# Branch B of a hybrid decoder layer: the odd head's keys copied out before the even head's split, and stored by ScalarE

## The chip, the core and the metric

The kernel runs on one NeuronCore of a Trainium2 chip. The engines are named as in the profile: PE is TensorE (PEld its weight loads), DVE is VectorE, ACT is ScalarE, POOL is GpSimd and SP is SyncE, which issues most of the DMA transfers; SPq and ACTq are the rows of DMAs issued by SP and by ACT. The metric is the device time of one execution in microseconds (us).

## The reference

One decoder layer over 1024 positions, 1024 wide, in f32. Branch B, where the change lies, is a latent attention with 8 heads:

```python
qb = (rmsnorm(cq, q_a_norm[l]) @ w_q_b[l]).reshape(B, S, N_HEADS_B, Q_HEAD_B)
kvb = (rmsnorm(ckv, kv_a_norm[l]) @ w_kv_b[l]).reshape(B, S, N_HEADS_B, KV_HEAD_B)
q_nope, q_rope = qb[..., :QK_NOPE], rope(qb[..., QK_NOPE:], positions)
k_nope, v_b = kvb[..., :QK_NOPE], kvb[..., QK_NOPE:]
k_rope = rope(kr[:, :, None, :], positions)[:, :, 0, :]
out_b = mla_attention(q_nope, q_rope, k_nope, k_rope, v_b)
merged = jax.nn.sigmoid(g_a) * (out_a @ w_o_a[l]) + jax.nn.sigmoid(g_b) * (out_b @ w_o_b[l])
x = x + rmsnorm(merged @ w_out[l], post_norm_mix[l])
h2 = rmsnorm(x, pre_norm_mlp[l])
y = jnp.square(jax.nn.relu(h2 @ w_up[l])) @ w_down[l]
x = x + rmsnorm(y, post_norm_mlp[l])
```

A head has 64 key columns of its own (`k_nope`) and 32 rotary ones that all heads share; scores are causal and scaled, and each softmax is over all earlier positions.

## The kernel before

Every f32 matrix is split into two parts, a high part (a cast on ACT, L83) and the rest (a subtraction, L84, mostly on DVE), and a product is three matmuls: L89 and L91 with the high part of the left operand, L90 with its low part. Tiles are 128 partitions by 512 or 1024 columns.

The order of work is the program text, reordered: the tile framework schedules each engine's row of instructions beforehand with a time model of its own (`schedule_with_timeline_sim=True`), and it puts in the waits. On the chip each engine then takes its row strictly in order. So a line moved in one function can move rows on every engine, and an instruction that waits holds up all that stand behind it on its engine.

In branch B `head_k` makes the keys of a pair of heads with one product: partitions 0 to 63 of the PSUM bank are the even head's keys, 64 to 127 the odd head's. The even head's half is split in place into `bkh` (ACT) and `bkl` (DVE). The odd head's half has to change partitions, so it goes through DRAM: ACT copies it into a `tmp` tile, a DMA stores that in `KN`, and `head_k` of the odd head loads `KN` into the low partitions of its `bkl` (L725) and splits it there (a cast on ACT, a subtraction on DVE). The shared rotary keys come by DMA too (`bkh<-krh`, `bkl<-krl`, L710). `tmp` has three buffers, shared with the query products (`scaled`, L252) and the gate products (`gate_out`, L450, stored to DRAM as `gate<-tmp`):

```python
def tmp():
    return tl(p1, [P, 512], F32, "tmp", 3)
```

PSUM is shared out by tags: `F` has one bank (gate products, and queries and keys of heads 1 to 7), `big` two tiles of two banks (scores, value projection, and queries and keys of head 0, `two_halves`), `T` two banks (transposed probabilities), `O` one. A tile of a tag can be written only when the one before it in the same buffer has been read.

A head's attention goes in steps `s` of two blocks of 128 queries: `attn_b_front` makes scores (L768 to L772), their maximum (L775, L776) and `e`, the exponentials (ACT, L778), which POOL divides by their sum (L781); `attn_b_back` of the step before transposes `e` (L797), splits it (`bth`, `btl`) and multiplies by the values (L805 to L808). Head h+1's keys and queries are made in step 2 of head h. Gate products (24 matmuls of 512 columns each) stand between as work that waits for little:

```python
NGATES = (3, 1, 2, 2, 2, 3, 3, 0)
```

After head 7 comes `merge`; it loads stored gates (`sg<-gate`, L910) and takes their sigmoid on ACT (L911), two of them already near the end of head 6. Exponential and sigmoid need different function tables on ACT, and an ACT_TABLE_LOAD row stands where they alternate.

Of the kernel before, what the change touches and what calls it, by code (L numbers as in the profile page):

```python
# [55 lines left out]
def layer(tc, t):  # L56
    nc = tc.nc
# [16 lines left out]
    def tl(p, shape, dt, tag, bufs=None):  # L74
        n_tiles[0] += 1
        kw = dict(tag=tag, name=f"{tag}_{n_tiles[0]}")
        if bufs is not None:
            kw["bufs"] = bufs
        return p.tile(shape, dt, **kw)

    def hilo(hi, lo, src, eng=None):

        a = nc.scalar.copy(out=hi, in_=src)  # L83
        return a, (eng or nc.vector).tensor_tensor(out=lo, in0=src, in1=hi.bitcast(F32), op=ALU.subtract)  # L84

    def mm3(out, lhs, rhs, first, last, chain=False):

        (lh, ll), (rh, rl) = lhs, rhs
        nc.tensor.matmul(out, lhsT=lh, rhs=rh, start=first, stop=False, skip_group_check=chain)  # L89
        nc.tensor.matmul(out, lhsT=lh, rhs=rl, start=False, stop=False, skip_group_check=chain)  # L90
        return nc.tensor.matmul(out, lhsT=ll, rhs=rh, start=False, stop=last, skip_group_check=chain)  # L91
# [138 lines left out]
    def tmp():  # L230
        return tl(p1, [P, 512], F32, "tmp", 3)
# [15 lines left out]
    def fbank():  # L247
        return tl(pss, [P, 512], F32, "F", 1)
# [381 lines left out]
    for half in range(2):  # L630
        ps = pb[:, half * 512:half * 512 + 512]
# [58 lines left out]
    KN = [[tc.dram_tile([64, 512], F32, name=f"kn_{v}_{h}") for h in range(2)] for v in range(4)]  # L690

    def two_halves(h, mm, out):
        if h == 0:
            pb = big()
            banks = [pb[:, :512], pb[:, 512:]]
            for half in range(2):
                mm(half, banks[half])
            for half in range(2):
                out(half, banks[half])
        else:  # L700
            for half in range(2):
                ps = fbank()
                mm(half, ps)
                out(half, ps)

    def head_k(h):
        w = w_head[h][0]
        kh, kl = tl(b3, [P, S], F32R, "bkh", 2), tl(b3, [P, S], F32R, "bkl", 2)
        for z, d in ((KR[0], kh), (KR[1], kl)):
            nc.sync.dma_start(out=d.bitcast(F32)[64:128, :], in_=z.bitcast(F32)[64:128, :])  # L710

        def cols(half):
            return slice(half * 512, half * 512 + 512)

        def mm(half, ps):
            c = cols(half)
            mm3(ps, w, (ckvT[0][:, c], ckvT[1][:, c]), True, True)

        def split(half, x):
            hilo(kh[0:64, cols(half)], kl[0:64, cols(half)], x[0:64])  # L720

        if h % 2:
            for half in range(2):
                x = kl.bitcast(F32)[:, cols(half)]
                nc.sync.dma_start(out=x[0:64], in_=KN[h // 2][half])  # L725
                split(half, x)
            return kh, kl

        def out(half, ps):
            split(half, ps)  # L730
            odd = tmp()[64:128]
            nc.scalar.copy(out=odd, in_=ps[64:128])
            nc.sync.dma_start(out=KN[h // 2][half], in_=odd)

        two_halves(h, mm, out)
        return kh, kl

# [108 lines left out]
    for i in range(NT):  # L846
        if i % 2 == 0:
            pb = big()
        ps = pb[:, (i % 2) * 512:(i % 2) * 512 + 512]
# [10 lines left out]
    for h in range(8):  # L860
# [12 lines left out]
        if h == 6:  # L873
# [4 lines left out]
            for c in range(EARLY):  # L878
                w = next_w()
                ps = fbank()  # L880
# [555 lines left out]
    for m, (p, g) in enumerate(steps):  # L1436
# [3 lines left out]
        ps = A if p in (1, 6, 7, 4) else B  # L1440
# [86 lines left out]
```

## Time and profile before

| | |
|---|---|
| three runs | 1361.52, 1362.48, 1364.94 us, median 1362.48 |
| profiled execution | 1366.29 us, its span 1364.5 us |
| granted PE clock, mean of the span | 0.989 |
| busy: PE, PEld, DVE, ACT, POOL | 97%, 80%, 58%, 50%, 32% |
| branch B of the attention | about 250 to 530 us of the span |

The profiled execution is 3.81 us longer than the median of the runs, and 1.79 us of it lie outside the span. Busy time of PE is that of modelled, pipelined matmuls. A group's last column in the profile names what ended the idle time ahead of it.

### The profile page before, as it was taken

What the parts mean: (1) busy time and instruction counts of PE and PEld (TensorE: products, weight loads), DVE (VectorE), ACT (ScalarE), POOL (GpSimd) and SP (SyncE); (2) the same over time, 40 slices, a digit from 0 to 9 for tenths busy, and PEclk for the clock granted to TensorE, in tenths of its full rate; (3) what the DMA queues carried; (4) which work ended last, traced back from release to release, by engine and by line L of the source; (5) the groups of instructions that cost most, each with busy time, mean ns of one, the idle gap of its engine ahead of it and who ended that gap; (6) DMA issues with size and microseconds to landing.
All of it is one profiled execution on the core that took longest, in us unless ns stands there. A gap on an engine that the chain in (4) does not pass through costs nothing.

```text
span 1364.5 us, 17800 instructions
## 1 busy us (share of the span) xinstructions
PE 1324.5 (97%) x6254; PEld 1085.2 (80%) x6254; DVE 794.7 (58%) x1248; ACT 678.7 (50%) x1181; POOL 433.2 (32%) x450
## 2 busy tenths in 40 slices
PE   9999999999999998999998899999999999999997
PEld 6887888788888876777886688888887888888886
DVE  5779745467666557874466544334434774567673
ACT  6476543356556455553343645555545434433541
POOL 3465501143333321223135186566545000000020
PEclk9999999999999998999999899999999999999999
DMA  8534342533334256874222254444346972357342
GB/s 306 144 93 119 122 127 76 149 104 101 88 91 111 80 159 185 248 237 167 97 93 85 94 178 159 156 162 159 128 162 237 409 255 93 108 182 238 103 136 97
DMA packets 90681, 206.00 MB, mean 151 GB/s; under 512 B 11360, under 2 KB 25312, under 8 KB 90592
## 3 DMA queue, kind: packets, MB, share of 16 engines
q1 hardware_dynamic: 89152, 200.15, 46.3%
q10 hardware_dynamic: 1440, 4.72, 0.9%
q8 instruction: 49, 0.80, 0.3%
q14 instruction: 40, 0.33, 0.1%
HBM read 141.65 MB, written 55.84 MB: 145 GB/s over the span
## 4 chain that ended last, share of the span: by engine, by line
PE 80%; DMA 6%; DVE 6%; ACT 3%; issue 2%; POOL 2%; SPq 0%; ACTq 0%; DVEq 0%; POOLq 0%
PE a L90 8%; PE a L91 8%; PE a L89 8%; PE c L89 5%; PE c L90 5%; PE c L91 5%; PE big L91 5%; PE big L89 5%; PE big L90 5%; PE F L90 4%; PE F L89 4%; PE F L91 4%; DMA raw<-w_o 2%; PE T L797 2%; PE big L771 1%
## 5 line engine op out<-in xcount | busy, mean ns | idle before, releaser
L83 ACT CAST whi<-raw 128x1024 fp32r<-128x1024 f32 (+1 forms) x78 | 78.6, 1009 | 99.5 <-PE big L90 29.1
L90 PE MATMUL F<-l,whi 128*128 128x512 f32 x260 | 103.5, 398 | 3.7 <-DVE l L84 3.7
L89 PE MATMUL F<-h,whi 128*128 128x512 f32 x260 | 104.2, 401 | 0.6 <-ACT h L83 0.4
L91 PE MATMUL F<-h,wlo 128*128 128x512 f32 x260 | 103.2, 397 | 0.0
L84 DVE TENSOR_TENSOR wlo<-raw,whi 128x1024 fp32r<-128x1024 f32 (+1 forms) x62 | 85.5, 1378 | 29.9 <-ACT whi L83 24.8
L996 POOL TENSOR_TENSOR raw<-raw,raw 128x512 f32<-128x512 f32 x48 | 63.5, 1324 | 121.5 <-DVE ol L84 95.8
L83 ACT CAST h<-h 128x1024 fp32r<-128x1024 f32 x50 | 51.7, 1049 | 98.2 <-PE a L90 36.1
L91 PE MATMUL big<-h,wlo 128*128 128x512 f32 x236 | 95.1, 403 | 5.4 <-DVE wlo L84 5.4
L89 PE MATMUL big<-h,whi 128*128 128x512 f32 x236 | 95.0, 404 | 2.2 <-DVE sg L918 1.4
L105 POOL TENSOR_SCALAR sums<-sums 128x1 f32<-128x1 f32 x8 | 3.4, 430 | 292.1 <-DVE sums L996 292.0
L90 PE MATMUL big<-l,whi 128*128 128x512 f32 x236 | 94.1, 399 | 0.0
L781 POOL TENSOR_SCALAR e<-e,bsm 128x128 f32<-128x128 f32 (+3 forms) x64 | 49.1, 770 | 138.2 <-DVE bsm L780 103.1
L84 DVE TENSOR_TENSOR l<-h,h 128x1024 fp32r<-128x1024 f32 x50 | 62.5, 1266 | 52.2 <-ACT h L83 52.1
L84 DVE TENSOR_TENSOR sl<-raw,sh 128x1024 fp32r<-128x1024 f32 x32 | 46.0, 1437 | 45.7 <-ACT sh L83 43.5
L778 ACT ACTIVATE e<-big,bsm 128x128 f32<-128x128 f32 (+3 forms) x64 | 47.6, 744 | 29.2 <-DVE bsm L776 20.3
L91 PEld LDWEIGHTS big<-h,wlo 128*128 128x128 f32 x236 | 45.4, 192 | 18.8 <-DVE wlo L84 9.3
L90 PEld LDWEIGHTS F<-l,whi 128*128 128x128 f32 x260 | 49.3, 190 | 13.1 <-DVE l L84 4.2
L84 DVE TENSOR_TENSOR btl<-T,bth 128x512 fp32r<-128x512 f32 (+1 forms) x80 | 50.1, 633 | 15.9 <-ACT bth L83 15.8
L83 ACT CAST h<-raw 128x1024 fp32r<-128x1024 f32 x27 | 28.2, 1051 | 62.1 <-PE c L90 24.4
L996 POOL TENSOR_TENSOR l<-h,l 128x512 f32<-128x512 f32 x32 | 57.6, 1800 | 0.7
L89 PEld LDWEIGHTS F<-h,whi 128*128 128x128 f32 x260 | 49.3, 190 | 10.5 <-ACT h L83 0.6
L91 PEld LDWEIGHTS F<-h,wlo 128*128 128x128 f32 x260 | 49.4, 190 | 9.8
(403 smaller groups left out, 4023.9 us busy)
## 6 DMA issues: line engine op xcount, KB each, us to landing
raw<-w_in SPq DMA_DIRECT2D x38, 512.0 KB, 3.6
raw<-w_up SPq DMA_DIRECT2D x32, 512.0 KB, 3.7
uc<-l SPq DMA_DIRECT2D x64, 256.0 KB, 3.1
h<-uc SPq DMA_DIRECT2D x31, 512.0 KB, 4.7
raw<-uc SPq DMA_DIRECT2D x25, 512.0 KB, 4.3
r<-w_down SPq DMA_DIRECT2D x24, 512.0 KB, 6.3
uc<-h SPq DMA_DIRECT2D x46, 256.0 KB, 2.2
gate<-tmp SPq DMA_DIRECT2D x32, 256.0 KB, 2.0
```

The lines of the kernel that those rows point to most:

```text
L83: a = nc.scalar.copy(out=hi, in_=src)
L84: return a, (eng or nc.vector).tensor_tensor(out=lo, in0=src, in1=hi.bitcast(F32), op=ALU.subtract)
L89: nc.tensor.matmul(out, lhsT=lh, rhs=rh, start=first, stop=False, skip_group_check=chain)
L90: nc.tensor.matmul(out, lhsT=lh, rhs=rl, start=False, stop=False, skip_group_check=chain)
L91: return nc.tensor.matmul(out, lhsT=ll, rhs=rh, start=False, stop=last, skip_group_check=chain)
L105: nc.gpsimd.tensor_scalar(out=out, in0=ss, scalar1=1.0 / dim, scalar2=EPS, op0=ALU.mult, op1=ALU.add)
L771: nc.tensor.matmul(o, lhsT=qh, rhs=kl[:, kc], start=False, stop=False)
L778: nc.scalar.activation(out=e[:, :nk].rearrange("p (a n) -> p a n", a=np_), in_=src, func=AF.Exp, bias=sm[:, 1:2], scale=SCALE_B, accum_out ...
L781: nc.gpsimd.tensor_scalar(out=e[:, :nk], in0=e[:, :nk], scalar1=sm[:, 3:4], scalar2=1.0, op0=ALU.mult, op1=ALU.mult)
L797: nc.tensor.transpose(pt[:, c0:c0 + P], es2[qi][:, kb * P:(kb + 1) * P], ident)
L996: eng.tensor_tensor(out=out, in0=a, in1=b, op=op)
```

## The change

In `out` of `head_k`, which runs for heads 0, 2, 4 and 6 and for two halves each (8 times), the odd head's copy now comes first, its store is issued by ACT in place of SP, and the even head's split comes last.

```diff
         def out(half, ps):
-            split(half, ps)
             odd = tmp()[64:128]
             nc.scalar.copy(out=odd, in_=ps[64:128])
-            nc.sync.dma_start(out=KN[h // 2][half], in_=odd)
+            nc.scalar.dma_start(out=KN[h // 2][half], in_=odd)
+            split(half, ps)
```

In the built programs this reorders some rows on every engine from head 0 to head 7, and a few in the up projection. Three places follow; the numbers in the names tell tiles of one name apart.

First place: ACT at head 0, from the cast of a key weight to the casts of head 0's queries. `big_2710` is the product of the keys of heads 0 and 1, `kn_0` and `kn_1` the stored halves, `bkl_3005` and `bkh_3004` the keys of head 1, `tmp_2740` and `tmp_2746` the two halves of head 0's queries. Before:

```order
L83 CAST wkh_4009<-wkr_4007 128x128
L83 CAST bkh_2706<-big_2710 64x512
L732 COPY tmp_2719<-big_2710 64x512
L83 CAST bkh_2706<-big_2710 64x512
L732 COPY tmp_2724<-big_2710 64x512
L83 CAST wqh_3303<-wqr_3301 128x256
L83 CAST bqh_2742<-tmp_2740 128x512
L83 CAST bqh_2748<-tmp_2746 128x512
L83 CAST whi_2813<-raw_2811 128x512
L83 CAST bkh_3004<-bkl_3005 64x512 x2
```

Of the change:

```order
L83 CAST wkh_4009<-wkr_4007 128x128
L731 COPY tmp_2717<-big_2710 64x512
L83 CAST bkh_2706<-big_2710 64x512
L732 DMA kn_0_2698<-tmp_2717 64x512
L731 COPY tmp_2722<-big_2710 64x512
L83 CAST bkh_2706<-big_2710 64x512
L732 DMA kn_1_2699<-tmp_2722 64x512
L83 CAST wqh_3303<-wqr_3301 128x256
L83 CAST bkh_3004<-bkl_3005 64x512
L83 CAST bqh_2742<-tmp_2740 128x512
L83 CAST bkh_3004<-bkl_3005 64x512
L83 CAST bqh_2748<-tmp_2746 128x512
```

The copies and stores moved ahead, and the casts of head 1's reloaded keys, which stood behind all of head 0's query casts, now stand one ahead of each.

Second place: PE around the value projection, which follows. `F_2810` is a gate product, `F_3014` the first half of head 1's queries, `big_2752` and `big_2764` head 0's scores of blocks 0 and 1, `big_2852` the value projection.

```order
+L772 MATMUL big_2752<-bkh_2706,bql_2743 128x128
+L772 MATMUL big_2764<-bkh_2706,bql_2743 128x256
 L89 MATMUL F_2810<-h_108,whi_2779 128x512
 L90 MATMUL F_2810<-l_109,whi_2779 128x512
 L91 MATMUL F_2810<-h_108,wlo_2780 128x512
+L89 MATMUL F_3014<-cqh_2167,wqh_2899 128x512
+L90 MATMUL F_3014<-cql_2168,wqh_2899 128x512
+L91 MATMUL F_3014<-cqh_2167,wql_2900 128x512
+L89 MATMUL F_3014<-cqh_2167,wqh_2899 128x512
+L90 MATMUL F_3014<-cql_2168,wqh_2899 128x512
+L91 MATMUL F_3014<-cqh_2167,wql_2900 128x512
 L89 MATMUL big_2852<-whi_2813,ckh_2169 128x512
```

Query matmuls of head 1 that stood behind twelve of the value projection now follow the gate product directly, in the same single bank of `F`. The same happens further on between the gate products `F_3113` and `F_3147`, where four score matmuls (`big_2915`) stood between:

```order
 L771 MATMUL big_2903<-bkl_2707,bqh_2742 128x384
 L772 MATMUL big_2903<-bkh_2706,bql_2743 128x384
-L89 MATMUL F_3113<-h_110,whi_2848 128x512
-L90 MATMUL F_3113<-l_111,whi_2848 128x512
 L91 MATMUL F_3113<-h_110,wlo_2849 128x512
+L89 MATMUL F_3147<-h_110,whi_3116 128x512
+L90 MATMUL F_3147<-l_111,whi_3116 128x512
 L768 MATMUL big_2915<-bkh_2706,bqh_2742 128x512
```

The last matmul of one gate product and the first of the next are neighbours now.

Third place: ACT at the end of head 6. `e_5323` and `e_5338` are the exponentials of its blocks 6 and 7 (scores `big_5312` and `big_5327`), `sg` the gates for `merge`, `T_5343` and `T_5352` transposes of blocks 4 and 5, `bqh_5308` the queries of head 7. Before:

```order
L778 ACTIVATE e_5323,bsm_5320<-big_5312,bsm_5320 128x896
L778 ACTIVATE e_5338,bsm_5335<-big_5327,bsm_5335 128x1024
L817 COPY bos_5272<-O_5246 128x256
L83 CAST bth_5348<-T_5343 128x512
L83 CAST bqh_5308<-tmp_5306 128x512
L83 CAST bth_5357<-T_5352 128x512
L911 ACT_TABLE_LOAD
L911 ACTIVATE sg_5914<-sg_5914 128x1024
L911 ACTIVATE sg_5962<-sg_5962 128x1024
L83 CAST whi_5422<-raw_5420 128x1024
L778 ACT_TABLE_LOAD
L778 ACTIVATE e_5561,bsm_5558<-big_5553,bsm_5558 128x128
```

Of the change:

```order
L911 ACT_TABLE_LOAD
L911 ACTIVATE sg_5914<-sg_5914 128x1024
L778 ACT_TABLE_LOAD
L778 ACTIVATE e_5323,bsm_5320<-big_5312,bsm_5320 128x896
L911 ACT_TABLE_LOAD
L911 ACTIVATE sg_5962<-sg_5962 128x1024
L83 CAST bqh_5308<-tmp_5306 128x512
L817 COPY bos_5272<-O_5246 128x256
L83 CAST bth_5348<-T_5343 128x512
L83 CAST bth_5357<-T_5352 128x512
L778 ACT_TABLE_LOAD
L778 ACTIVATE e_5338,bsm_5335<-big_5327,bsm_5335 128x1024
```

Both sigmoids moved ahead of `e_5338`, one of them ahead of `e_5323`, and four table loads stand where two did.

## Rows read from the trace of the kernel before

**Rows 1.** The page's busy time of each engine.
```profile
PE 1324.5 (97%) x6254; PEld 1085.2 (80%) x6254; DVE 794.7 (58%) x1248; ACT 678.7 (50%) x1181; POOL 433.2 (32%) x450
```

**Rows 2.** Stretches: length, busy PE, PEld, DVE, ACT, POOL, clock, DMA share, GB/s.
```profile
250.00:275.00 25.00, 21.72 (x91) 17.09 (x90) 10.99 (x24) 11.49 (x22) 3.25 (x3) 0.93 0.57 144
275.00:300.00 25.00, 24.93 (x125) 20.13 (x126) 15.33 (x29) 11.76 (x23) 10.31 (x7) 1.00 0.29 95
325.00:500.00 175.00, 175.00 (x1042) 150.54 (x1041) 104.52 (x239) 98.57 (x209) 59.36 (x55) 1.00 0.37 102
```

**Rows 3.** Waits of PE, 245 to 580 us: total, times, longest.
```profile
PE big L768 <- DVE tmp L252: 2.7, 1, 2.7
```

**Rows 4.** Timeline at head 0: start, us, engine, line, instruction, idle before.
```profile
249.97 0.58 ACT L83 CAST bkh<-big 64x512 fp32r<-64x512 f32 x1
...
251.30 0.58 ACT L732 COPY tmp<-big 64x512 f32<-64x512 f32 x1 [0.75 <-DVE bkl L84]
...
253.44 2.80 SPq L733 DMA_DIRECT2D kn<-tmp  x2
...
260.25 1.10 SPq L725 DMA_DIRECT2D bkl<-kn  x2
260.33 0.69 DVE L252 TENSOR_TENSOR tmp<-big,cs 128x512 f32<-128x512 f32 x1 [3.30 <-DMA kn<-tmp]
...
261.07 0.38 PE L768 MATMUL big<-bkh,bqh 128*128 128x256 f32 x1 [2.71 <-DVE tmp L252]
...
262.61 0.51 PE L89 MATMUL F<-h,whi 128*128 128x512 f32 x1
...
262.79 0.62 ACT L83 CAST bkh<-bkl 64x512 fp32r<-64x512 f32 x1 [0.60 <-DMA bkl<-kn]
```

**Rows 5.** Transfers issued at 252.79, at 253.44, and ACT's own: KB, us to landing.
```profile
bkl<-krl SPq DMA_DIRECT2D x1, 256.0 KB, 7.2
kn<-tmp SPq DMA_DIRECT2D x1, 128.0 KB, 6.8
x<-x ACTq DMA_DIRECT2D x8, 512.0 KB, 2.6
```

**Rows 6.** Timeline where one gate product follows another.
```profile
285.10 0.56 DVE L775 TENSOR_REDUCE bsm<-big 128x1 f32<-128x384 f32 x1 [2.70 <-PE big L772]
...
285.36 0.40 PE L91 MATMUL F<-h,wlo 128*128 128x512 f32 x1
...
285.80 0.69 DVE L450 TENSOR_TENSOR tmp<-F,rstdB 128x512 f32<-128x512 f32 x1
...
286.63 0.47 PE L89 MATMUL F<-h,whi 128*128 128x512 f32 x1
```

**Rows 7.** End of head 6: PE, ACT, POOL and SP, and the landing of `sg`.
```profile
471.44 0.45 PE L768 MATMUL big<-bkh,bqh 128*128 128x448 f32 x1
...
476.54 0.81 SPq L910 DMA_DIRECT2D sg<-gate  x2
...
476.81 0.93 PE L797 MATMUL T<-ident,e 128*128 128x128 f32 x7
...
477.15 1.11 ACT L778 ACTIVATE e<-big,bsm 128x1024 f32<-128x1024 f32 x1
...
477.86 2.12 POOL L781 TENSOR_SCALAR e<-e,bsm 128x896 f32<-128x896 f32 x2 [4.92 <-DVE bsm L780]
477.93 0.45 PE L89 MATMUL F<-h,whi 128*128 128x512 f32 x1
...
480.12 1.28 ACT L911 ACT_TABLE_LOAD   x1
481.42 1.06 ACT L911 ACTIVATE sg<-sg 128x1024 f32<-128x1024 f32 x1
...
483.45 0.28 PE L805 MATMUL O<-bth,h 128*128 128x256 f32 x1
...
sg<-gate SPq DMA_DIRECT2D x1, 256.0 KB, 3.0
```

## Prediction

> **What bounds the kernel now.** I read the page's busy times first: PE is busy 97% of the span, no other engine above 60% [rows 1]. So a change counts by what it does to PE's idle time and to its clock. The stretches say where there is anything to win: between 325 and 500 us, most of branch B, PE is busy in every microsecond at full clock, and nothing there can get faster without less matmul work, which the change doesn't bring. At head 0, 250 to 275 us, PE lacks 3.28 us, and the clock granted there is 0.93; 275 to 300 us lacks 0.07 us [rows 2]. The list of PE's waits names the stall of head 0: one wait of 2.7 us for the query product's eviction (L252) [rows 3]. The timeline then shows what that eviction waited for [rows 4]. SP issued the stores of the odd head's keys at 253.44, the first landed 6.8 us later [rows 5], and the eviction, which needs the `tmp` buffer of that store, began at 260.33 after 3.30 us of idle. PE got its `big` tile back at 261.07 and reached the next gate product at 262.61 [rows 4].
>
> **What the change removes there.** The first copy can begin where the cast began, at 249.97, lasts 0.58 us, the cast behind it as long [rows 4], and ACT's issue then stands at about 251.2, where SP's was at 253.44. ACT's own stores land in 2.6 us for 512 KB [rows 5]; the store before took 6.8 us behind 256 KB transfers that took 7.2 [rows 5]. The new one lands between 253.8 and 258.0. The eviction's other conditions hold before 257, as PE waited for nothing else there, so it no longer waits: the 2.7 us wait goes, and with it the gate eviction behind it can be early. A store on ACT costs ACT eight issues that are short and stand in its idle time.
>
> **What takes its place.** The reload of `kn` (L725) is still SP's, in its queue behind `bkl<-krl`, which was issued at 252.79 and landed 7.2 us later, at 260.0 [rows 5]. It takes the queue place of the old store, which landed at 260.24 (253.44 + 6.8). If the store lands only at 258.0, the reload adds what it took before, 260.25 to the cast at 262.79, 2.54 us [rows 4]: 260.5. Both ends agree on 260.2 to 260.6; if the 256 KB transfers did not hold it back, it could land at 253.8 + 2.54 = 256.3. I take 260.5, since those bytes have to pass whoever stores `kn`. ACT's new order puts the cast of this reload ahead of head 0's first query cast. So PE's first scores of head 0, which started before 258 in the old order, wait for 260.5 + two casts of 0.62 = 261.75, and DVE's gate eviction behind the split of the reload for 260.5 + 0.62 + 0.69 + 0.69 = 262.5. PE reaches the gate product at 262.6, as before; two L772 matmuls that were then done are still to come, about 0.3 us. So a stall of 2.7 us for the store is exchanged for one of nearly 4 us for the reload, at the same end. The clock goes with it: 0.93 over 25 us is 1.75 us, kept. **Head 0: +0.3**, between -5.2 (reload at 256.3: 3.28 of idle and 1.75 of clock gone, most of a microsecond of handover left, 0.3 added) and +2.3 (reload no earlier than before, 262.8).
>
> **Two handovers of one bank.** In the new PE row the first query product of head 1 follows a gate product directly in the one bank of `F`. What that costs is seen in rows 6 when the score matmuls between are thought away: the last L91 starts at 285.36, the eviction at 285.80 when it ends, the next L89 at 286.63: 1.27 us from matmul to matmul. Without a wait it is 0.23 (24 gate matmuls from 477.93 to 483.45 [rows 7]). Loss 1.04 us; before, twelve value matmuls (2.8 us) stood there and hid it. At the second place, `F_3113` to `F_3147`, the score matmuls that hid all but 0.2 us are gone too, and on DVE the maximum of `big_2903` (0.56 us [rows 6]) stands ahead of the eviction; one gate matmul of 0.23 runs beside it. Loss 1.04 + 0.56 - 0.23 = 1.37, less the 0.2 of before: 1.15. **+2.2 together**; not below 1.0 for the two, since an eviction of 0.69 us can't be hidden by work that waits for its bank, and not above 3.4 (should a tile of the value projection also be evicted late, twice 0.6).
>
> **End of head 6.** Two sigmoids, and with them two more table loads, stand ahead of `e_5338` now. I count from the issue of `sg<-gate`, which SP made at 476.54, when PE was at its last query matmul of head 7; the order puts it at the same matmul. ACT: both halves of the first `sg` there at 0.4 + 3.0 = 3.4 (the pair's issues take 0.81 [rows 7]); then four table loads at 1.28 (5.1), two sigmoids at 1.06 (2.1), `e_5323` and `e_5338` at about 1.0 and 1.11 (2.1), four casts and copies between, taken as 0.5 each (2.0): `e_5338` ends at 14.7. PE: from 471.44 to 483.45 it did 12.0 us in which the same scores and gate products stand; less six query matmuls (1.4), plus 22 transposes and value matmuls at 0.1 (0.93 us for seven, which the next instruction cuts to 0.68): 12.8, from its query's end at 0.4, and some 0.3 for `btl_5349`, whose cast is late too: it wants the tile of `e_5338` at 13.5. It waits 1.2; then the transposes of `e_5338` wait for POOL's division (2.12 us for two, 1.1 for one) and 0.3 for the reciprocal, less 0.5 of scores: 0.9. With the 0.3: **+2.4**. Between 0 (without the two extra loads `e_5338` would be done at 12.1; two microseconds of error in ACT's chain remove the stall) and 4.4 (two microseconds the other way).
>
> Of the table load the trace shows 1.28 us, and the sigmoid starts 0.02 us after it [rows 7]. The Trainium skill (ScalarE: Activation LUTs, What ACT_TABLE_LOAD costs) puts a switch at about 2.66 us, a load of 1.283 and a drain of 1.38. The trace agrees with its load and has no drain in this place; by the page's figure, an estimate, `e_5338` would end 5.5 us later and the sum would be +10.4.
>
> **Everything else** I cost at nothing: the copies ahead of the splits in heads 2, 4, 6 delay keys by 0.58 us that are needed a step later, under a PE that has other rows; SP loses eight issues it didn't lack; the few moved rows of the up projection exchange neighbours. If that cover is gone, some 0.6 us each.
>
> **Sum.** 0.3 + 2.2 + 2.4 = +4.9 us. The profiled execution would go from 1366.29 to 1371.2, the median of the runs, which is 3.81 lower, from 1362.48 to 1367.4, 0.36% up. What a measurement can tell here from no change is 0.3%, 4.1 us: slower begins at 1366.6, faster ends at 1358.4.
>
> **The rivals.**
> 1. *Head 0 clears.* The reload is not held back, because the stores no longer stand in SP's queue. For it: the old store's 6.8 us were nearly all queue. Against it: 256 KB ahead of it took 7.2 us. From a landing before 257 on, PE doesn't stop: -5.2 instead of +0.3, with +2.2 and +2.4 kept 1362.48 - 0.6 = 1361.9, not slower.
> 2. *The table loads stay hidden.* ACT's chain at head 6 is 2 us shorter than I add up, for example as `sg` lands sooner or casts overlap. Then +2.5: 1365.0, no change to be told.
> 3. *The clock falls once more.* Idle time of 2 us and more at a new place (head 6) brings the granted clock down as at head 0, where 2.7 us did and 1.75 us were lost: +6.7, 1369.2.
> 4. *A switch costs more than its row.* A drain beside each of the four loads, hidden in the rows before: `e_5338` later by four times the drain, 1372.9. It is the page's rule above; the rows speak against it.
> 5. *The change does nothing.* PE's new waits fall into others, and head 0 ends as before: 1362.5. Against it stand two handovers that have no other work between them.
>
> **How the numbers follow.** Forecast 0.40, rival 1 0.14, rival 2 0.20, rival 3 0.13, rival 4 0.03, rival 5 0.10. Time 1367.4. The range goes from 1360.8 (rival 1 with a microsecond of error) to 1371.0 (rival 3 with nearly two); the forecast's own is 1365.5 to 1369.5. Slower by over 0.3%: 0.29 of the forecast's 0.40, 0.13 of rival 3, 0.03 of rival 4, a little of 2: 0.47. Faster: a part of rival 1 and of 5, 0.08. The same: 0.45.
>
> **What would show it.** In the changed profile: the store issued near 251 by ACT and landed before 258; no wait of L252 for it; instead ACT idle until about 260.5 for the reload and PE's first scores of head 0 after 261; a wait of the first L89 on a query product for L252 or L450 of DVE, about 0.8 to 1.1 us, at each of the two handovers; four table loads near the end of head 6, and there a PE wait for ACT's `e` and one for POOL's, 2 us together, where PE had none. The prediction is wrong if PE stays fully busy around 480 us, if the reload lands before 257, or if a new stall stands in 300 to 470 us.

## The result, and the profile after

The changed kernel took 1371.96 us in the median of five runs (1368.13 to 1373.23), the kernel before 1362.83 us in five runs beside it: a ratio of 1.0062, 95% interval 1.0045 to 1.0078. It is slower by 9.1 us; 1367.4 was forecast, and the range ended at 1371.0. The profiled execution of the change took 1373.23 us, its span 1371.4; that of before took 1366.29.

The page's line of busy times, to be read beside [rows 1]:

```profile
PE 1324.4 (97%) x6254; PEld 1084.1 (79%) x6254; DVE 792.7 (58%) x1248; ACT 680.2 (50%) x1183; POOL 431.2 (31%) x450
```

PE's busy time is the same to 0.1 us and the span is 6.9 us longer, so the difference is PE waiting. (The granted clock, over the whole span, has the same mean in both, 0.990 and 0.989.) The view of stretches says where (columns as in [rows 2]):

```profile
250.00:275.00 25.00, 20.99 (x87) 16.37 (x86) 10.00 (x21) 9.35 (x18) 3.21 (x3) 0.93 0.54 155
275.00:300.00 25.00, 23.20 (x115) 18.46 (x114) 13.96 (x29) 11.81 (x24) 9.84 (x7) 1.00 0.24 74
325.00:470.00 145.00, 145.00 (x871) 125.06 (x871) 88.92 (x201) 81.00 (x179) 50.59 (x47) 1.00 0.36 98
470.00:500.00 30.00, 27.35 (x151) 22.83 (x149) 14.64 (x34) 19.30 (x34) 9.01 (x10) 0.94 0.38 104
```

Head 0 (250 to 275 us) is short of 4.0 us of PE where it was short of 3.28, 275 to 300 us of 1.8 where it was 0.07, and the end of head 6, without a gap before [rows 2], lacks 2.65 us. There the granted clock is 0.94 as well: 30 us x 0.06 = 1.8 us more. Between 325 and 470 us nothing is lost in either kernel.

The list of PE's waits, 245 to 580 us (total, times, longest), beside [rows 3]:

```profile
PE big L768 <- ACT bqh L83: 3.0, 1, 3.0
...
PE O L805 <- ACT bth L83: 2.6, 2, 2.2
...
PE F L89 <- ACT l L83: 1.1, 1, 1.1
...
PE F L89 <- DVE tmp L450: 0.8, 1, 0.8
```

The wait for L252 is gone, as the change meant, and the scores (L768) wait 3.0 us for the cast of the query instead. The two handovers of the bank are the 0.8 us (before the first query product of head 1) and the 1.1 us: the list puts the latter down to a cast on ACT, but the eviction of the bank (L450) ended only 0.07 us before that cast did, so the handover alone would have made nearly the same wait. The timeline of the changed kernel at head 0 shows why the scores wait, beside [rows 4]:

```profile
249.75 0.52 ACTq L732 DMA_DIRECT2D kn<-tmp  x1
...
251.69 0.46 ACTq L732 DMA_DIRECT2D kn<-tmp  x1
...
255.14 3.43 SPq L725 DMA_DIRECT2D bkl<-kn  x2
255.41 1.29 DVE L252 TENSOR_TENSOR tmp<-big,cs 128x512 f32<-128x512 f32 x2 [2.44 <-PE big L91]
...
258.99 0.62 ACT L83 CAST bkh<-bkl 64x512 fp32r<-64x512 f32 x1 [3.40 <-DMA bkl<-kn]
259.51 0.61 ACT L83 CAST bqh<-tmp 128x512 fp32r<-128x512 f32 x1
...
260.18 0.33 PE L768 MATMUL big<-bkh,bqh 128*128 128x128 f32 x1 [2.98 <-ACT bqh L83]
```

DVE evicts both queries from 255.41, as soon as their product is done, so `tmp` was free. Their cast could have begun near 256 us; it stands in ACT's row behind the cast of the reload, which landed at 258.99. At the end of head 6 the timeline of ACT, SP and PE is, beside [rows 7]:

```profile
474.62 1.51 SPq L910 DMA_DIRECT2D sg<-gate  x3
...
479.88 1.28 ACT L911 ACT_TABLE_LOAD   x1 [3.60 <-DMA sg<-gate]
481.17 1.06 ACT L911 ACTIVATE sg<-sg 128x1024 f32<-128x1024 f32 x1
482.25 1.28 ACT L778 ACT_TABLE_LOAD   x1
483.54 1.01 ACT L778 ACTIVATE e<-big,bsm 128x896 f32<-128x896 f32 x1
...
484.66 1.28 ACT L911 ACT_TABLE_LOAD   x1
...
485.95 1.06 ACT L911 ACTIVATE sg<-sg 128x1024 f32<-128x1024 f32 x1
487.69 1.07 ACT L83 CAST bth<-T 128x512 fp32r<-128x512 f32 x2
...
488.32 0.39 PE L805 MATMUL O<-bth,h 128*128 128x256 f32 x1 [2.22 <-ACT bth L83]
488.78 1.28 ACT L778 ACT_TABLE_LOAD   x1
489.94 0.56 PE L805 MATMUL O<-bth,h 128*128 128x256 f32 x1
490.07 1.11 ACT L778 ACTIVATE e<-big,bsm 128x1024 f32<-128x1024 f32 x1
```

ACT stands for 3.60 us behind a sigmoid that waits for its transfer, the last 1.5 of them with the exponential of 896 columns ready (its maximum was done at 478.35); four table loads follow, and PE waits 2.22 us for a cast behind the second sigmoid. All of PE's waits from 470 to 500 us:

```profile
PE O L805 <- ACT bth L83: 2.2, 1, 2.2
PE O L807 <- DVE btl L84: 0.2, 1, 0.2
PE big L768 <- ACT e L778: 0.2, 1, 0.2
```

The matmul of 0.56 us at 489.94 took 0.28 before: PE at the lower of its two clocks (granted 0.50 from 490 to 492 us).

To compare executions I use the length of branch B on PE: from the last transposes of the query's tables (L544) to the wait of a gate product (L90) for the output projection's inputs. Before and after, two lines of each timeline:

```profile
247.51 1.03 PE L544 MATMUL T<-ident,tbs 128*128 128x128 f32 x8
...
510.27 0.50 PE L90 MATMUL F<-l,whi 128*128 128x512 f32 x1 [2.28 <-DVE l L84]
```
```profile
246.59 1.03 PE L544 MATMUL T<-ident,tbs 128*128 128x128 f32 x8
...
517.35 0.50 PE L90 MATMUL F<-l,whi 128*128 128x512 f32 x1 [1.88 <-DVE l L84]
```

That is 262.76 us before and 270.76 after: 8.0 of the 9.1 us lie here. What lies behind differs between executions: from there to a wait of 2.33 us in the up projection (765.72 us before, 774.54 after) it is 255.4 us before, 257.2 after, and 254.8 in a second execution of the same rows (`e7` below, 518.94 to 773.71).

### The profile page after: what moved, and what is told of

Same layout as the page of the kernel before. It is cut to its first block, busy times and chain, and to the rows that moved or that the text cites. A ratio compares the mean times of both kernels' runs of the same rounds, so it can differ in the third digit from the quotient of the medians.

```text
span 1371.4 us, 17779 instructions
## 1 busy us (share of the span) xinstructions
PE 1324.4 (97%) x6254; PEld 1084.1 (79%) x6254; DVE 792.7 (58%) x1248; ACT 680.2 (50%) x1183; POOL 431.2 (31%) x450
## 4 chain that ended last, share of the span: by engine, by line
PE 79%; DMA 8%; DVE 5%; ACT 4%; issue 2%; POOL 1%; SPq 1%; ACTq 0%; DVEq 0%; POOLq 0%
PE a L90 8%; PE a L91 8%; PE a L89 8%; PE c L91 5%; PE c L90 5%; PE c L89 5%; PE big L89 4%; PE big L91 4%; PE big L90 4%; PE F L89 4%; PE F L90 4%; PE F L91 4%; DMA raw<-w_o 3%; PE T L797 2%; DMA sg<-gate 2%
## 5 line engine op out<-in xcount | busy, mean ns | idle before, releaser
L90 PE MATMUL F<-l,whi 128*128 128x512 f32 x260 | 102.8, 396 | 3.1 <-DVE l L84 3.1
L90 PE MATMUL big<-l,whi 128*128 128x512 f32 x236 | 93.8, 397 | 0.0
L84 POOL TENSOR_TENSOR wlo<-raw,whi 128x1024 fp32r<-128x1024 f32 x16 | 38.3, 2395 | 81.5 <-ACT whi L83 76.7
L775 DVE TENSOR_REDUCE bsm<-big 128x1 f32<-128x128 f32 (+3 forms) x64 | 47.8, 753 | 24.9 <-PE big L772 23.9
L90 PEld LDWEIGHTS F<-l,whi 128*128 128x128 f32 x260 | 49.3, 190 | 12.6 <-DVE l L84 3.6
```

The lines of the kernel that those rows point to most:

```text
L775: nc.vector.reduce_max(out=sm[:, 0:1], in_=src, axis=AX.XY)
```

## The experiments

All in one table: median, ratio to the kernel before with its 95% interval (not the quotient of the two medians), difference of the medians to the kernel before measured beside it, length of branch B, PE's idle time in 250 to 325 us, and idle time with granted clock in 470 to 500 us (the last four from the profiled execution).

```
kernel                      median   ratio to before (95%)    to before  branch B  idle 250-325  idle, clock 470-500
before                      1362.83                              -        262.76     3.47         0.00  1.00
the change                  1371.96  1.0062 (1.0045-1.0078)    + 9.1      270.76     6.26         2.65  0.94
e1 order only               1370.54  1.0061 (1.0039-1.0083)    + 7.8      272.40     7.11         1.99  0.94
e2 store only               1358.82  0.9976 (0.9961-0.9991)    - 4.0      259.35     2.13         0.00  1.00
e3 sigmoids held            1365.95  1.0023 (1.0012-1.0034)    + 3.2      266.50     6.85         0.00  1.00
e4 first handover held      1369.91  1.0053 (1.0036-1.0069)    + 7.1      272.65     6.13         2.32  0.89
e5 reload held              1363.56  1.0004 (0.9990-1.0018)    + 1.4      263.25     1.97         2.95  1.00
e6 reload, sigmoids held    1357.76  0.9963 (0.9948-0.9978)    - 4.4      259.07     1.92         0.00  1.00
e7 the change again         1372.95  1.0078 (1.0059-1.0096)    +10.8      271.93     6.16         2.30  0.89
e8 e6, late rotary keys     1357.38  0.9968 (0.9956-0.9981)    - 4.7      257.35     0.33         0.00  1.00
e9 change, late rotary keys 1372.25  1.0080 (1.0061-1.0099)    +10.2      270.07     6.71         2.70  1.00
```

**Which half of the change costs?** `e1` has the new order of the code and SP's store, `e2` the old order and ACT's store.

```diff
             split(half, ps)
             odd = tmp()[64:128]
             nc.scalar.copy(out=odd, in_=ps[64:128])
-            nc.sync.dma_start(out=KN[h // 2][half], in_=odd)
+            nc.scalar.dma_start(out=KN[h // 2][half], in_=odd)
```

> Only the order of the code is changed (copy, store, split), the store stays on SP. Two theories of where the 9 us of the change come from. A (mine): the rows that the scheduler moved, not the engine that issues the store. B: the issue of eight stores from ACT, which stands in ACT's row between casts. Here the rows of PE are those of the change but for some 200 lines between heads 1 and 5, with the same two bank handovers in heads 0 and 1 and the same four table loads at the end of head 6. By A the time is that of the change or a little more, since the reload of head 1's keys waits for a store that is late again in SP's queue: 1370 to 1375 us, with a PE wait of 2 us and more near 488 us. By B it is that of the kernel before, 1361 to 1365.

> Only the engine of the store is changed, the code's order stays (split, copy, store). The rows of PE, DVE and POOL are word for word those of the kernel before; ACT has eight stores more and SP eight fewer. By A (moved rows cost) it is as before or faster: the stores land some 3 us earlier than 260.2, the wait of 2.7 us for L252 in head 0 becomes shorter or goes, and with it perhaps the low clock behind it: 1358.5 to 1363. By B (issues on ACT cost) it is 1368 to 1373.

`e1` took 1370.54 us (ratio 1.0061, 1.0039 to 1.0083), `e2` 1358.82 (0.9976, 0.9961 to 0.9991). Theory B falls: the eight issues on ACT cost nothing, and alone they gain 4 us. All of the loss is in the moved rows. The two halves don't add, though: in the new order the store from ACT gains nothing that can be told (1371.96 against 1370.54), so the new order costs 7.8 us with SP's store and 13.1 with ACT's. The timeline of `e2` at head 0:

```profile
252.24 0.50 ACTq L733 DMA_DIRECT2D kn<-tmp  x1
...
259.30 0.69 DVE L252 TENSOR_TENSOR tmp<-big,cs 128x512 f32<-128x512 f32 x1 [1.95 <-DMA kn<-tmp]
...
260.05 0.38 PE L768 MATMUL big<-bkh,bqh 128*128 128x256 f32 x1 [1.36 <-DVE tmp L252]
```

The first store was issued at 252.24 and landed 7.0 us later, 259.2; the query eviction follows at 259.30, where it stood at 260.33 [rows 4]. PE's wait is 1.36 us where it was 2.71, and the clock stays at 1.00 where it was 0.93 over 25 us: 1.35 + 1.75 of the 3.4 us by which branch B is shorter.

**The end of head 6.** `e3` is the change with the first two sigmoids held behind the last exponential of head 6; 34 lines of PE's row differ, none ahead of that place. (`exps`, here and below, is a dictionary that keeps instructions to hold others behind.)

```diff
-            nc.scalar.activation(out=e[:, :nk].rearrange("p (a n) -> p a n", a=np_), in_=src, func=AF.Exp,
+            exps[h, i] = nc.scalar.activation(out=e[:, :nk].rearrange("p (a n) -> p a n", a=np_), in_=src, func=AF.Exp,
...
-            nc.scalar.activation(out=sg, in_=sg, func=AF.Sigmoid)
+            with tc.issue_after(exps[6, 7].ins) if half == 0 and c < 2 else nullcontext(): nc.scalar.activation(out=sg, in_=sg, func=AF.Sigmoid)
```

> The change, with the first two sigmoids of the merge held behind the last exponential of head 6, as they stood before; 34 lines of PE's row differ, all after the end of head 6. By A, with the size that the trace shows at that place (2.62 us of PE idle from 485.8 to 491.3 and 1.70 us of clock from 488 to 494), the time falls by 4.3 us against the change, to 1366.5 to 1369, and PE is busy throughout 470 to 505 us at full clock. By the rival that the wait only moves (to the loads of the output projection, 6 us later in the row) it stays at 1370 to 1373.

It took 1365.95 us, against the kernel before 5.9 less than the change, and branch B is 4.3 shorter. The stretch of `e3`'s profile:

```profile
470.00:500.00 30.00, 30.00 (x181) 25.81 (x180) 18.87 (x41) 20.16 (x39) 10.72 (x10) 1.00 0.46 129
```

The stall and the low clock are both gone and have not gone elsewhere. The median falls by more than this one profile shows; with the two intervals the 5.9 us are uncertain by some 2.7. The clock behind the stall differs between executions, as `e7` shows: the changed kernel once more, with the same rows on every engine.

> The changed kernel once more (two blanks in the source, the same rows on every engine), for how much of its profile is the execution's own. From the last transpose of head 0's tables to the first wait of the output projection's load the change took 270.8 us, before 262.8: expected again 270.8 within 0.7, with the stall of head 6 and the low clock behind it. In the output projection (543 to 632 us) the change's profile had 9.7 us of PE waits for weights, the other five 6 to 7: expected 6 to 7, which would make that part chance. Median 1369.5 to 1373.

It took 1372.95 us. Branch B was 271.93, a little outside what was expected, and the stretch reads:

```profile
470.00:500.00 30.00, 27.70 (x141) 22.88 (x141) 14.45 (x33) 19.22 (x34) 9.51 (x10) 0.89 0.37 104
```

A smaller stall (2.30 us idle) and a larger loss of clock: 30 x 0.11 = 3.3 us, an estimate, as all of these are. In the output projection this execution has 8.4 us without PE work from 543 to 632 us, the change 9.9 in the same stretch: not the 6 to 7 expected (before: 6.2). Over the six profiles with a stall here (the change, `e1`, `e4`, `e5`, `e7`, `e9`) the clock cost 1.8, 1.8, 3.3, 0, 3.3 and 0 us. The length of the stall doesn't decide it: the longest, 2.95 us in `e5`, cost none.

**The handovers of the bank.** `e4` holds head 1's first query product behind the fourth value product, as it stood before; in the rows the second handover goes with it.

```diff
-        mm3(ps, (ckvT[0][:, c], ckvT[1][:, c]), w, True, True)
+        exps['v', i] = mm3(ps, (ckvT[0][:, c], ckvT[1][:, c]), w, True, True)
...
-                mm3(ps, wslice(w, k), (cqT[0][:, k, cols], cqT[1][:, k, cols]), k == 0, k == 1)
+                with tc.issue_after(exps['v', 3].ins) if (h, half, k) == (1, 0, 0) else nullcontext(): mm3(ps, wslice(w, k), (cqT[0][:, k, cols], cqT[1][:, k, cols]), k == 0, k == 1)
```

> The change, with head 1's first query product held behind the fourth value product, as it stood before; in the rows the second handover of the bank is gone too, and the end of head 6 is as in the change. By A the waits of 0.78 us near 269 and of 1.11 and 0.32 us near 287 go, and 2 us of time with them: 1369 to 1371. By the rival (the bank's handover is hidden by what waits anyway) the time stays that of the change, 1371 to 1373, with other waits in 265 to 300 us. Head 0's stall of 3 us for the reload stays in both.

1369.91 us, within what was expected of A, but the profile speaks for the rival. PE's waits, 245 to 330 us:

```profile
PE big L768 <- ACT bqh L83: 3.0, 1, 3.0
PE big L89 <- ACT e L778: 2.7, 1, 2.7
PE big L89 <- DVE h L84: 0.4, 1, 0.4
```

The waits of the handovers (0.78, 1.11 and the small ones behind them) are gone, and a wait of 2.7 us has come for the exponentials of head 0, which free the `big` tile of the value products. Idle time in 250 to 325 us is 6.13 us against 6.26, the clock there is lower, and branch B is longer by 1.9. So the first handover cost little of its own: it stood in front of the late exponentials of a head 0 whose scores were late. That the median is 2 us lower than the change's, with this profile, is within the scatter of both and settles nothing.

**Head 0.** `e5` holds the splits of the reload behind both query casts, the place that they had before; `e6` does this and what `e3` does.

```diff
-            hilo(kh[0:64, cols(half)], kl[0:64, cols(half)], x[0:64])
+            with tc.issue_after(exps['q', 0, 1].ins) if h == 1 else nullcontext(): hilo(kh[0:64, cols(half)], kl[0:64, cols(half)], x[0:64])
...
-            hilo(qh, ql, x)
+            exps['q', h, half] = hilo(qh, ql, x)[0]
```

> The change, with the splits of head 1's reloaded keys held behind both query casts of head 0 on ACT, as they stood before. In the rows the two bank handovers of heads 0 and 1 go with it (the first query product of head 1 stands behind value products again); the end of head 6 is as in the change. Theory: what costs at head 0 is the reload cast ahead of the query casts, not the transfers themselves, since the stores landed by 258.1 us in the change. Then PE's stall of 2.98 us there goes to a few tenths, the 1.7 us of clock behind it too, and the small waits from 269 to 312 us (2.8 us): the change less some 7, 1363.5 to 1366, with the wait and the low clock of head 6 kept. Rival: the query eviction waits for the store's tmp buffer again (in the run with the store alone it waited until 259.3 us): a stall of 1 to 3 us near 259 us, 1366 to 1369.

> The change with both holds: reload splits behind head 0's queries, the first two sigmoids behind the last exponential of head 6. If the two costs add, it is the run with the reload held less 4.3: 1358 to 1361.5, faster than the kernel before (1362.8) and about where the store alone stands (1358.8). If the moved rows in heads 1 to 5 carry a cost of their own (small waits and changes between kinds of matmuls, 1.1 us by the difference of the two profiles), it stays above the store alone by that: 1359.5 to 1361. If the stalls only move, 1363 or more.

`e5` took 1363.56 us (ratio 1.0004, 0.999 to 1.0018), against the kernel before 7.7 less than the change: the place of two splits undoes nearly all of the loss, though the stall of head 6 is still there (2.95 us). The hold also brings rows of PE and DVE in heads 0 and 1 back, the two handovers among them, so it shows the splits together with the rows that the scheduler moved with them; `e4` had the handovers alone. `e6` took 1357.76 (0.9963, 0.9948 to 0.9978), 5.8 less than `e5`: the two costs add. Heads 1 to 5 keep their moved rows in `e6`, and its branch B is 0.3 us shorter than that of `e2`, which has the old rows: those moves cost nothing. What is left at head 0 in `e6`, two lines of its timeline:

```profile
259.12 0.69 DVE L450 TENSOR_TENSOR tmp<-F,rstdB 128x512 f32<-128x512 f32 x1 [1.38 <-PE big L772]
...
259.87 0.50 PE L89 MATMUL F<-h,whi 128*128 128x512 f32 x1 [1.58 <-DVE tmp L450]
```

The gate eviction began at 259.12, when the second store landed: issued at 251.79, 7.3 us, so at 259.1. The row names PE's L772 as its releaser, which was done by 258.3 us; the store's buffer fits.

**What makes a store of 128 KB take 7 us on a queue of its own?** `e8` is `e6` with SP's two 256 KB transfers of head 1's rotary keys issued behind the reload of `kn`; no row of another engine differs. `e9` makes the same move in the change.

```diff
-        for z, d in ((KR[0], kh), (KR[1], kl)):
-            nc.sync.dma_start(out=d.bitcast(F32)[64:128, :], in_=z.bitcast(F32)[64:128, :])
+        def keys_r(z, d): return nc.sync.dma_start(out=d.bitcast(F32)[64:128, :], in_=z.bitcast(F32)[64:128, :])
+        if h != 1: keys_r(KR[0], kh); keys_r(KR[1], kl)
...
-                nc.sync.dma_start(out=x[0:64], in_=KN[h // 2][half])
+                exps['r', h] = nc.sync.dma_start(out=x[0:64], in_=KN[h // 2][half])
                 split(half, x)
-            return kh, kl
+            with tc.issue_after(exps['r', h].ins): h == 1 and (keys_r(KR[0], kh), keys_r(KR[1], kl)); return kh, kl
```

> The run with both holds, and SP issues the two 256 KB transfers of head 1's rotary keys behind the reload of kn rather than ahead of the store; every other row on every engine is the same. Tells what made the stores take 5.3 and 7.3 us on a queue that holds nothing else. If it is the bytes of other queues on the same DMA engines: the second store lands 2 us or more earlier than 259.1 us, the gate eviction (L450) no longer waits for its buffer, PE's 1.58 us near 259.9 goes to 0.3 or less, and the median falls to 1355.5 to 1357.5. If it is the issue from ACT or the store's own size, landing and stall stay, 1357 to 1359.

> The same move of the two transfers in the changed kernel itself, all rows of PE the same. The prediction took the reload of head 1's keys as held back by these bytes whoever stores kn, and put the stall of head 0 on it. If so, stores and reload come 2 us or more earlier, PE's 2.98 us near 260 falls to 1 us or less and the low clock behind it goes in most executions: 1367.5 to 1370 with all else of the change kept. If the reload is late for another reason (SP's waits for the store, its own 128 KB), the stall stays at 2.5 to 3 us and the time at 1370 to 1373.

The landing of the second store (transfers issued near 251.8 us), first in `e6`, then in `e8`:

```profile
kn<-tmp ACTq DMA_DIRECT2D x1, 128.0 KB, 7.3
```
```profile
kn<-tmp ACTq DMA_DIRECT2D x1, 128.0 KB, 4.7
```

2.6 us less, with nothing changed in ACT's queue: the bytes on SP's queue held it. The eviction is at 257.72 in `e8`, PE's wait is gone, idle time in 250 to 325 us is 0.33 us and branch B 1.7 us shorter. The median is 1357.38 (0.9968, 0.9956 to 0.9981), 0.4 below `e6` and not to be told from it; the two profiled executions are 0.3 apart, so what branch B gained was lost again behind it. The Trainium skill (DMA: Bandwidth & Descriptors, Queues, rings and completion order) says that the queues of SP and ACT are rows on the same 16 DMA engines, served in turn, and that the increment which reports a transfer as done lands only after every earlier write of that DMA engine, across its queues. The two landings, 7.3 and 4.7 us, fit either; which of the two rules makes the 2.6 us no run here shows.

`e9` didn't gain: 1372.25 us. The timeline of its head 0:

```profile
257.29 0.62 ACT L83 CAST bkh<-bkl 64x512 fp32r<-64x512 f32 x1 [5.19 <-DMA bkl<-kn]
257.94 0.68 DVE L84 TENSOR_TENSOR bkl<-bkl,bkh 64x512 fp32r<-64x512 f32 x1 [5.12 <-ACT bkh L83]
258.55 1.27 DVE L252 TENSOR_TENSOR tmp<-big,cs 128x512 f32<-128x512 f32 x2
...
260.08 0.33 PE L768 MATMUL big<-bkh,bqh 128*128 128x128 f32 x1 [3.04 <-ACT bqh L83]
```

The reload lands 1.7 us earlier (257.29 against 258.99), but in this kernel's rows on DVE the split of the reload stands ahead of the query evictions, which ran at 255.41 in the change, and on ACT both casts of the reload stand ahead of both query casts. So the queries now wait for the reload on two engines, and the stall is the same. The run shows that the reload comes earlier; it doesn't show what that alone would be worth in the change's own rows.

## Why the prediction was wrong

- **The sign, the places and the chains were right.** Store issued by ACT, no wait for L252, ACT idle until the reload at 258.99 (260.5 was taken; this execution runs 0.92 us ahead of that of before), a stall of 2.98 us for the exchanged one of 2.71 + 0.30, four table loads at head 6, PE fully busy in between: as listed. Only PE's waits at head 6 were others than listed.
- **Head 0 (+0.3) and the two handovers (+2.2).** Together +2.5 forecast; idle time in 250 to 325 us rose by 6.26 - 3.47 = 2.8, and the change without head 6's share (`e3`) is 3.2 slower in the median. The sum held, and as waits the handovers came near their price (0.78 and 1.11 us for 1.04 and 1.15). As separate causes they did not hold: `e4` shows them as part of head 0's delay, and `e5` removes all of it with one hold.
- **End of head 6 (+2.4): the step that failed.** This term was too small. In the medians the place costs 5.9 us (the change to `e3`) and 5.8 (`e5` to `e6`), each uncertain by some 2.7 by the intervals. What the term had at nothing is the clock behind the stall, which stood apart as rival 3, with a chance of 0.13 and 1.75 us: in four of six profiles with this stall the clock fell, and over the six it cost 0 to 3.3 us, 1.7 in the mean, beside 2.0 to 2.95 us of idle time. With 5.9 in place of 2.4 the sum is 1362.5 + 0.3 + 2.2 + 5.9 = 1370.9; measured 1372.0. Rival 3 itself, at 1369.2, would still have been 2.8 us short. The row of head 0 had shown a clock loss as large as half the stall [rows 2].
- **The idle time at head 6 (2.65 us for 2.4) is right in part by luck.** The chain on ACT was added up rightly: from the landing of `sg` to the end of `e_5338` it took 11.3 us (479.88 to 491.18), as forecast. But `sg` landed 5.3 us after its first issue (474.62), where 3.4 was taken, which alone would have added 1.9. Against that, the wait for `e` came to 0.18 us where 1.2 was forecast, and the one for POOL (0.9) didn't come: PE had already waited 2.22 us for `bth`, where 0.3 was taken for that split, and then ran at the lower clock. In `e9`, whose rows on PE are the same, the waits are 0.88 for `bth`, 0.97 for `e` and 0.62 for POOL, nearer to the list.
- **What the profile doesn't account for.** Of branch B's 8.0 us, 2.8 + 2.65 are idle time, 1.8 is clock, and the later load waits 0.4 less; 1.2 us remain. By the same sum as much remains in `e5` and nothing in `e6`, but `e3`, without the stall of head 6, keeps 0.8, and `e4`, with it, 0.3. So the rest doesn't sort by that stall, and no row names it; this stays open, as does what the medians show at head 6 beyond idle time and clock.
- **"Everything else at nothing" held** for heads 1 to 5 (`e6`). Rival 1 was true of other kernels: head 0 clears by the earlier store in part where the rows stay (`e2`), and wholly with the reload held and the rotary keys late (`e8`). Its price in the prediction doesn't come out of its own terms: -3.28 - 1.75 + 0.3 is -4.7 and not -5.2, so rival 1 and the lower end of the range stand some 0.5 us too low, which decided nothing. Rival 4, a drain beside each table load, is out: at each of the four loads the work behind follows by 0.01 us or so (479.88 + 1.28, 481.17), and the three that waited for no transfer follow the work before them by 0.02. The 2.66 us a switch of the Trainium skill (ScalarE: Activation LUTs, What ACT_TABLE_LOAD costs) don't appear here.

## What to carry to other kernels

An edit of two lines held a gain of 4 us (the store off a loaded queue) and, with that store, a loss of 13 us (9.1 + 4.0: the rows that the scheduler moved because of it); the two were told apart by a version that changes the resource and leaves every other row alone. Read a new order for instructions that wait for a transfer and now stand ahead of ready work on an in-order engine: holding two splits and two sigmoids, with the rows that moved back with them, undid the whole loss here and made the change the faster kernel (1357.8). A new stall on PE in a stretch that had none is to be priced with the clock behind it, not beside it: here 0 to 3.3 us behind stalls of 2.0 to 2.95.

## What was not expected of the hardware

- The same stall was followed by 1.8 us of lost clock in one execution of the change, by 3.3 in another (`e7`), and by none in `e9`, whose rows on PE are the same (470 to 500 us, the table). The mean clock of a run's span, which is on record for every run, goes with this: 0.9886 over the 17 runs with these rows on PE (the change, `e7`, `e9`) and 0.9904 over the 12 of `e3`, an estimate of 2.4 us (from `e5` to `e6` it is 0.7). Among the 17 the lower clock goes mostly with the longer time (0.993 at 1368.18 us, 0.986 at 1375.62), but not always (0.990 at both 1368.13 and 1373.23), so the scatter of 5 us between runs of the change is explained only in part.
- A 128 KB store alone on ACT's queue took 7.3 us, and 4.7 once two 256 KB transfers of SP's queue were issued behind it: a second queue takes the issue off SP, but not the bytes out of the way.
